# A delta rule's decay matrices as fp32r products of a fixed mask and split decays, four tiles in one matmul

## The chip, the cores and the metric

The kernel runs on one core of a Trainium2 chip. The metric is the device time of one execution in microseconds (us), here the median of 3 runs. The core has TensorE (PE: matmuls; PEld: its weight loads), VectorE (DVE), ScalarE (ACT), GpSimd (POOL) and SyncE (SP, which only issues DMAs). Each engine works through its own list of instructions in order; engines wait for one another by semaphores.

## The reference

A two-layer encoder over two sequences of 256 tokens each. Each layer has three branches side by side: latent attention, a gated linear recurrence (RG-LRU) and a gated delta rule with 4 heads, forward and backward; then a feed-forward part. The change lies in the delta rule alone. For each head and direction the log decays `g` of a chunk of 64 tokens are summed, and the exponentials of their differences scale the products of keys and queries:

```python
g = jnp.cumsum(chunks(g), axis=-1)
decay = jnp.exp(jnp.where(tril, g[..., :, None] - g[..., None, :], -jnp.inf))
A = jnp.where(strict, jnp.einsum('nbhid,nbhjd->nbhij', kb, k) * decay, 0.0)
T = lax.linalg.triangular_solve(eye + A, jnp.broadcast_to(eye, A.shape), left_side=True,
                                lower=True, unit_diagonal=True)
attn = jnp.einsum('nbhid,nbhjd->nbhij', q, k) * decay
q_dec = q * jnp.exp(g)[..., None]
```

The kernel works on tiles of 128 tokens (four tiles for both sequences) instead of chunks of 64.

## The kernel before

**Work and order.** Activations lie transposed, 128 channels on the partitions and 512 tokens (both sequences) in the columns. Nearly all of the time goes to products with weights, each done as three fp32r matmuls of 128x512 (`wh`,`wl` and `hh`,`hl` are the high and low parts of weight and activation). The weights come by DMA in pieces of 128x1024 (`raw`); ACT makes `wh` and DVE makes `wl`. Beside this stream the delta rule, the recurrence and the attention run as generators. PE's order is fixed when the program is built: a `Driver` keeps a virtual clock that each emitted matmul moves on, and a generator that has yielded a time (table `SLACK`) is taken up again when the clock has passed it. The orders of DVE, ACT, POOL and SP are made by the framework's scheduler from the whole program, so that they move when the program does.

**The part that changes** is the first half of `solve(h)`, run for 4 heads in each of 2 layers. For each direction DVE scales a strict triangular mask by the decays of the four tiles (`gw`, 128x512, L1317), and PE multiplies each tile of it with the inclusive mask, in fp32, four 128x128 products into `gdn_z` (L1326). ACT takes the exponential (`E`). For the decay of the queries DVE fills a third `gw` with the decays (two operations of 128x256, L1335) and PE does four more fp32 products into `gdn_eg` (L1340). The tile `gw` has two buffers.

**What follows in a head.** The products of keys and queries (`gdn_gram`, L1352) are scaled on DVE into `B`. The 16x16 diagonal blocks of `B` go to POOL by way of DRAM (`cb`, `dl`, `Lb`), where 30 operations (`xt`, `X`, L1381 and L1382) invert them; the result goes back by way of DRAM (`dx`) into `W`, which DVE transposes (L1392, L1393). Products on PE then join the blocks to 32 (`gdn_l16`: two stages, `W` added to at L1421 and transposed at L1422), to 64 (`gdn_l32`, two stages) and to 128 columns (`gdn_l64`, two stages); a trace names all of these `gdn_l`. POOL copies the parts of `W` into `XF` and `Y` (L1439, L1438), DVE copies the last part of `Y` (L1475), and the recurrence over tiles (`gdn_rec`) uses `Y`. The next head's diagonal blocks are inverted on POOL while this head is joined.

**What shares the engines with it.** In the stretch of head 1, the RG-LRU puts long scans and products on DVE (`rs`, `ru`, `xc`, `gsq`), and splits `xc` into `xch` (POOL, recorded at L308) and `xcl` (DVE, L298). Two helpers record most of the operations: L220 all matmuls, L292, L295, L298 and L301 those of DVE and POOL.

Of the kernel before, what the change touches and what calls it, by code (L numbers as in the profile page):

```python
# [8 lines left out]
F32 = mybir.dt.float32  # L9
F32R = mybir.dt.float32r  # L10
# [3 lines left out]
ALU = mybir.AluOpType  # L14
# [4 lines left out]
P = 128  # L19
# [60 lines left out]

CC = {}
_n = 0
for _name, _w in [("ident", 128), ("ones", 128), ("incf", 128), ("incb", 128), ("strf", 128),
                  ("strb", 128), ("sel1", 2), ("sel2", 4), ("sel4", 8), ("off16", 64)]:
    CC[_name] = (_n, _w)
    _n += _w
NCC = _n


def constants():  # L90
# [144 lines left out]
def _body(es, tc, nc, xT, cT, wall, wmod, pvec, fng, cst, rope, xinit, yT, dbg):  # L235
    V, A, G = nc.vector, nc.scalar, nc.gpsimd
    drv = Driver()
    PE = Tensor(nc.tensor, drv)
    depth = pvec.shape[1]

    cp = es.enter_context(tc.tile_pool(name="const", bufs=1))
    sp = es.enter_context(tc.tile_pool(name="small", bufs=1))
# [8 lines left out]

    def fill(pool, size):
        return pool.tile([P, size // 4], F32, name="fill", tag="fill", bufs=1)
    fill(sp, 160)


    cs = cp.tile([P, NCC], F32, name="cs")
    nc.scalar.dma_start(cs, cst)

    def C(name):  # L260
        o, w = CC[name]
        return cs[:, o:o + w]
# [5 lines left out]
    ident, ones = C("ident"), C("ones")  # L268
# [351 lines left out]
    xs, h = [], {}  # L620
    start = ExitStack()
    stp = start.enter_context(tc.tile_pool(name="start", bufs=1))
    c_raw = stp.tile([P, 8, 32], F32, name="c_raw")
    nc.sync.dma_start(c_raw, cT)
    t1 = stp.tile([P, 8, 32], F32, name="c_t")
# [8 lines left out]
    for k in range(8):  # L634
        t = xp.tile([P, T], F32, name="x", tag="x")
# [8 lines left out]
    for k in range(8):  # L644
        t = stp.tile([P, T], F32, name="sq", tag="t", bufs=4)
# [31 lines left out]
    for l in range(depth):  # L677
# [342 lines left out]
        for job in JOBS:  # L1020
# [91 lines left out]
            elif k == "out":  # L1112
                d, g = ix
# [25 lines left out]
            elif k == "down":  # L1139
                d, g = ix  # L1140
# [16 lines left out]
                t = x1[d]  # L1157
# [29 lines left out]
class GDN:  # L1187
# [16 lines left out]
    def gates(self, ab):  # L1204
# [14 lines left out]
        fl = "p a b -> p (a b)"  # L1219
        self.softplus(self.g.rearrange(fl), al.rearrange(fl), 32)  # L1220
        V.tensor_tensor(self.g, self.g, nea, ALU.mult)
        yield SLACK["softplus"]

        pc = self.aux_tile((P, 4, 16), "gates")
# [76 lines left out]
    def solve(self, h):  # L1301
# [10 lines left out]
        gt = self.g.rearrange("p t e -> p e t")  # L1312


        def scaled(mask, cols):
            w = g2.tile([P, 4, P], F32, name="gw", tag="gw", bufs=2)
            V.tensor_tensor(w, mask.unsqueeze(1).to_broadcast([P, 4, P]), self.bc(cols, P), ALU.mult)  # L1317
            return w

        ws = [scaled(C(strict[d]), gt[:, 4 * d + h, :]) for d in range(2)]  # L1320
        yield SLACK["ws"]
        E = []
        for d in range(2):
            pz = self.aux_tile((P, 4, P), "gdn_z")
            for t in range(4):
                PE.matmul(pz[:, t, :], ws[d][:, t, :], C(inc[d]), start=True, stop=True)  # L1326
            e = g2.tile([P, 4, P], F32, name="E", tag="E", bufs=4)
            A.activation(e, pz, AF.Exp)
            E.append(e)
            if d == 0:  # L1330
                yield SLACK["z"]

        w = g2.tile([P, 4, P], F32, name="gw", tag="gw", bufs=2)
# [347 lines left out]
```

## Time and profile before

| what | value |
|---|---|
| median of 3 runs | 2039.64 us (2038.04 to 2040.38) |
| the profiled execution | 2038.05 us |
| its span in the trace | 2036.3 us |
| PE busy | 1980.2 us, 97% |
| DVE, ACT, POOL busy | 1249.8, 808.7, 254.7 us |
| mean granted TensorE clock | 0.983 |

The span runs from the first to the last instruction; the execution's own time is 1.75 us longer. Busy time counts instructions that do work; an engine can also stand between them, waiting for another one. The granted clock is the share of the full TensorE clock (2.4 GHz) that PE had.

### The profile page before, as it was taken

How to read it: one execution, taken by the hardware profiler on the slowest of the kernel's cores; microseconds unless marked ns; L12 is line 12 of the kernel's file. 1: busy time of each engine (PE TensorE's matmuls, PEld its weight loads, DVE VectorE, ACT ScalarE, POOL GpSimd, SP SyncE). 2: the span in 40 equal slices, each digit the busy share in tenths (PEclk: the TensorE clock that was granted, in tenths of full speed). 3: DMA queues.
4: the chain of work that ended last, by engine and by line, in shares of the span. 5: the costliest groups of instructions: out<-in, count | busy, mean ns of one | idle time of the engine just before them, and what ended most of it. 6: DMA issues, size and time to landing. Idle time of an engine off the chain costs nothing.

```text
span 2036.3 us, 28679 instructions
## 1 busy us (share of the span) xinstructions
PE 1980.2 (97%) x11179; PEld 1561.3 (77%) x11179; DVE 1249.8 (61%) x2354; ACT 808.7 (40%) x1259; POOL 254.7 (13%) x519
## 2 busy tenths in 40 slices
PE   9999989999999999999999999799999999999998
PEld 4777756767887778888878777577778878888887
DVE  5675767744466766662367757785544667666434
ACT  3454355422333434442234534553323344444322
POOL 1100252222100100000011003523130010000000
PEclk9999989999999999999999999899999999999999
DMA  7232433334335343344334224333442533333333
GB/s 300 83 94 63 118 86 100 108 112 117 88 117 194 114 135 102 94 142 153 114 109 108 59 77 114 92 114 85 127 111 82 207 104 102 95 94 104 94 95 112
DMA packets 114135, 229.94 MB, mean 113 GB/s; under 512 B 52304, under 2 KB 57552, under 8 KB 114000
## 3 DMA queue, kind: packets, MB, share of 16 engines
q1 hardware_dynamic: 107376, 219.98, 36.2%
q10 hardware_dynamic: 6624, 8.14, 1.2%
q8 instruction: 88, 1.44, 0.3%
q14 instruction: 47, 0.39, 0.1%
HBM read 221.00 MB, written 7.08 MB: 112 GB/s over the span
## 4 chain that ended last, share of the span: by engine, by line
PE 83%; DVE 5%; POOL 5%; DMA 3%; issue 2%; ACT 2%; SPq 1%; POOLq 0%; DVEq 0%; ACTq 0%
PE mm_up L220 24%; PE mm_down L220 12%; PE mm_gate L220 11%; PE mm_br L220 6%; PE mm_out L220 4%; PE mm_in L220 3%; PE mod L220 3%; PE mm_z L220 2%; PE mm_gk L220 2%; PE mm_gv L220 2%; POOL xt L292 2%; POOL X L298 2%; PE mm_gq L220 2%; PE att_s L220 1%; PE gdn_rec L220 1%
## 5 line engine op out<-in xcount | busy, mean ns | idle before, releaser
L298 DVE TENSOR_TENSOR wl<-raw,wh 128x1024 fp32r<-128x1024 f32 x304 | 374.6, 1232 | 307.5 <-ACT wh L387 301.8
L387 ACT CAST wh<-raw 128x1024 fp32r<-128x1024 f32 x304 | 319.0, 1050 | 533.2 <-PE mm_down L220 126.9
L220 PE MATMUL mm_up<-hh,wh 128*128 128x512 f32 x704 | 276.4, 393 | 3.5 <-POOL hh L308 3.5
L220 PE MATMUL mm_up<-hl,wh 128*128 128x512 f32 x704 | 275.4, 391 | 0.0
L220 PE MATMUL mm_up<-hh,wl 128*128 128x512 f32 x704 | 275.0, 391 | 0.0
L301 DVE SCALAR_TENSOR_TENSOR cv<-mm_up,pv,cv 128x510 f32<-128x510 f32 x176 | 131.2, 748 | 68.5 <-ACT cv L550 65.4
L220 PEld LDWEIGHTS mm_up<-hh,wh 128*128 128x128 f32 x704 | 132.9, 189 | 38.0 <-issue 5.9
L220 PE MATMUL mm_gate<-hh,wh 128*128 128x512 f32 x384 | 160.6, 418 | 0.0
L220 PEld LDWEIGHTS mm_up<-hl,wh 128*128 128x128 f32 x704 | 132.9, 189 | 27.8 <-DVE hl L298 0.4
L220 PEld LDWEIGHTS mm_up<-hh,wl 128*128 128x128 f32 x704 | 132.9, 189 | 27.8
L220 PE MATMUL mm_gate<-hh,wl 128*128 128x512 f32 x384 | 150.2, 391 | 0.0
L220 PE MATMUL mm_gate<-hl,wh 128*128 128x512 f32 x384 | 149.9, 390 | 0.0
L220 PE MATMUL mm_down<-ah,wl 128*128 128x512 f32 (+1 forms) x396 | 144.8, 366 | 0.5 <-DVE wl L298 0.5
L220 PE MATMUL mm_down<-ah,wh 128*128 128x512 f32 (+1 forms) x396 | 144.9, 366 | 0.0
L220 PE MATMUL mm_down<-al,wh 128*128 128x512 f32 (+1 forms) x396 | 144.7, 365 | 0.0
L308 POOL TENSOR_SCALAR hh<-hn 128x256 fp32r<-128x256 f32 x64 | 34.0, 544 | 689.2 <-ACT hn L567 686.8
L550 ACT ACTIVATE cv<-mm_up,pv 128x512 f32<-128x512 f32 x88 | 68.5, 780 | 93.4 <-PE mm_up L220 93.4
L220 PEld LDWEIGHTS mm_gate<-hh,wh 128*128 128x128 f32 x384 | 72.2, 188 | 25.5 <-issue 12.5
L220 PEld LDWEIGHTS mm_gate<-hh,wl 128*128 128x128 f32 x384 | 72.1, 188 | 16.2
L220 PEld LDWEIGHTS mm_down<-ah,wl 128*128 128x128 f32 x396 | 74.7, 189 | 12.7 <-DVE wl L298 0.7
L220 PEld LDWEIGHTS mm_down<-ah,wh 128*128 128x128 f32 x396 | 74.7, 189 | 12.1
L220 PEld LDWEIGHTS mm_down<-al,wh 128*128 128x128 f32 x396 | 74.7, 189 | 12.0
(389 smaller groups left out, 3869.4 us busy)
## 6 DMA issues: line engine op xcount, KB each, us to landing
raw<-in_wall_dram SPq DMA_DIRECT2D x304, 512.0 KB, 3.6
raw<-in_wmod_dram SPq DMA_DIRECT2D x56, 512.0 KB, 3.6
mraw<-in_wmod_dram SPq DMA_DIRECT2D x16, 512.0 KB, 10.0
oraw<-in_wmod_dram SPq DMA_DIRECT2D x16, 512.0 KB, 7.3
hraw<-in_wmod_dram SPq DMA_DIRECT2D x16, 256.0 KB, 5.3
x<-in_xT_dram SPq DMA_DIRECT2D x8, 256.0 KB, 5.6
xr<-in_xT_dram ACTq DMA_DIRECT2D x8, 256.0 KB, 3.5
xdram<-x ACTq DMA_DIRECT2D x16, 128.0 KB, 2.5
```

What stands on the lines that cost most here:

```text
L220: return self.pe.matmul(out, lhsT, rhs, **kw)
L292: (eng or V).tensor_tensor(out, a, b, ALU.mult)
L298: (eng or V).tensor_tensor(out, a, b, ALU.subtract)
L301: V.scalar_tensor_tensor(out, a, s, b, op0, op1)
L308: G.tensor_scalar(hi, x, 1.0, 0.0, ALU.mult, ALU.add)
L387: A.copy(wh, raw)
L550: A.activation(dst, ps, AF.Identity, bias=bias, scale=w[lo])
```

## The change

The log decays `g` (128x32 for all heads) are split once in a layer into two fp32r parts, by two small operations on DVE; the high part takes the place of a tile that is free by then (`al_`). In `solve` the mask that is scaled is now the inclusive one, by each part (four DVE operations of 128x512 for a head). The other factor is the fixed strict mask, so one matmul of 512 columns does four tiles: two fp32r matmuls (high and low part) for `gdn_z` of a direction, and two of 256 columns with a matrix of ones for half of `gdn_eg`, from the same `gw`. Ones and strict masks are therefore needed in fp32r: they move to the end of the table of constants, come by a DMA of their own and are rounded into `mk` by one operation on POOL. The yields `z`, `gw` and `eg` are gone; `ws` is passed once in each direction.

```diff
@@ constants, _body
+    cs = cp.tile([P, NCC - NMASK], F32, name="cs")
+    nc.scalar.dma_start(cs, cst[:, 0:NCC - NMASK])
+    mk = cp.tile([P, NMASK], F32R, name="mk")
...
+    m_raw = stp.tile([P, NMASK], F32, name="m_raw")
+    nc.scalar.dma_start(m_raw, cst[:, NCC - NMASK:])
+    G.tensor_scalar(mk, m_raw, 1.0, 0.0, ALU.mult, ALU.add)
@@ gates
         V.tensor_tensor(self.g, self.g, nea, ALU.mult)
+        self.gs = [al.bitcast(F32R), sp.tile([P, 4, 8], F32R, name="g_l", tag="g_l")]
+        V.tensor_copy(self.gs[0], self.g)
+        self.sub(self.gs[1], self.g, self.f32(self.gs[0]))
         yield SLACK["softplus"]
@@ solve
-        ws = [scaled(C(strict[d]), gt[:, 4 * d + h, :]) for d in range(2)]
-        yield SLACK["ws"]
         E = []
+        pe = self.aux_tile((P, 4, P), "gdn_eg")
         for d in range(2):
+            ws = []
+            for x in self.gs:
+                w = g2.tile([P, 4, P], F32R, name="gw", tag="gw", bufs=2)
+                V.tensor_tensor(w, C(inc[d]).unsqueeze(1).to_broadcast([P, 4, P]),
+                                self.bc(self.f32(x).rearrange("p t e -> p e t")[:, 4 * d + h, :], P), ALU.mult)
+                ws.append(w)
+            yield SLACK["ws"]
             pz = self.aux_tile((P, 4, P), "gdn_z")
-            for t in range(4):
-                PE.matmul(pz[:, t, :], ws[d][:, t, :], C(inc[d]), start=True, stop=True)
+            for i, w in enumerate(ws):
+                PE.matmul(pz, C(strict[d], F32R), w, start=(i == 0), stop=(i == 1))
+            for i, w in enumerate(ws):
+                PE.matmul(pe[:, 1 - d::2, :], C("ones", F32R), w[:, 1 - d::2, :], start=(i == 0), stop=(i == 1))
             e = g2.tile([P, 4, P], F32, name="E", tag="E", bufs=4)
             A.activation(e, pz, AF.Exp)
             E.append(e)
-            if d == 0:
-                yield SLACK["z"]
-
-        w = g2.tile([P, 4, P], F32, name="gw", tag="gw", bufs=2)
-        for d in range(2):
-            V.tensor_tensor(w[:, 1 - d::2, :], self.ones.unsqueeze(1).to_broadcast([P, 2, P]),
-                            self.bc(gt[:, 4 * d + h, 1 - d::2], P), ALU.mult)
-        yield SLACK["gw"]
-        pe = self.aux_tile((P, 4, P), "gdn_eg")
-        for t in range(4):
-            PE.matmul(pe[:, t, :], w[:, t, :], C(inc[1 - t % 2]), start=True, stop=True)
```

The change also moves work on the engines whose order the scheduler makes. Line numbers after the change are 1 to 6 higher at most places.

The first place is on DVE, in the stretch of head 1 of layer 0, where `W` (head 0's inverse blocks) is transposed. Before:

```order
L298 TENSOR_TENSOR wl<-raw,wh 128x1024
L298 TENSOR_TENSOR xcl<-xc,xch 128x512
L301 SCALAR_TENSOR_TENSOR rs<-rm,rs 128x512
L911 MEMSET ra 128x2
L1335 TENSOR_TENSOR gw<-cs,g__763 128x2x128
L910 MEMSET rs 128x2
L1335 TENSOR_TENSOR gw<-cs,g__763 128x2x128
L1317 TENSOR_TENSOR gw<-cs,g__763 128x512
L1392 STREAM_TRANSPOSE W<-W 128x128
L1393 STREAM_TRANSPOSE W<-W 128x128
L1317 TENSOR_TENSOR gw<-cs,g__763 128x512
```

and now:

```order
L301 TENSOR_TENSOR wl<-raw,wh 128x1024
L1393 STREAM_TRANSPOSE W<-W 128x128
L301 TENSOR_TENSOR xcl<-xc,xch 128x512
L1394 STREAM_TRANSPOSE W<-W 128x128
L304 SCALAR_TENSOR_TENSOR rs<-rm,rs 128x512
L917 MEMSET ra 128x2
L1330 TENSOR_TENSOR gw<-cs,al__766 128x512
L916 MEMSET rs 128x2
L1330 TENSOR_TENSOR gw<-cs,g_l 128x512
L1330 TENSOR_TENSOR gw<-cs,al__766 128x512
L1330 TENSOR_TENSOR gw<-cs,g_l 128x512
```

The `gw` that finish head 1 stood ahead of the two transposes; now the first two of the four, which are head 1's second direction, stand behind both (the last two are head 2's first).

The second place is PE's order for head 1, which uses those `gw`. Before, from the second `gdn_z`:

```order
L220 MATMUL gdn_z<-cs,gw 128x128 x4
L220 MATMUL mod<-raw,csil 32x512 x2
L220 MATMUL mm_g<-hh_460,wh 128x512
...
L220 MATMUL mm_g<-hh_550,wl 128x512
L220 MATMUL gdn_eg<-cs,gw 128x128 x4
L220 MATMUL mm_b<-xch,wh 128x512
```

and now, from the first:

```order
L221 MATMUL gdn_z<-gw,mk 128x512 x2
L221 MATMUL gdn_eg<-gw,mk 128x2x128 x2
L221 MATMUL mm_g<-hh_452,wh 128x512
...
L221 MATMUL mm_g<-hh_554,wl 128x512
L221 MATMUL gdn_z<-gw,mk 128x512 x2
L221 MATMUL gdn_eg<-gw,mk 128x2x128 x2
L221 MATMUL mm_b<-xch,wh 128x512
```

Both products of the second direction now stand where `gdn_eg` alone stood, behind the last `mm_g` of that piece.

The third place is POOL, at head 1's inversion (`xt` and `X`), where `xch` is a part of the RG-LRU that DVE's `xcl` waits for. Before, `xch` stood behind the whole inversion:

```order
L298 TENSOR_TENSOR X<-X,xt 128x8x2
L292 TENSOR_TENSOR xt<-Lb,X 128x8
L298 TENSOR_TENSOR X<-X,xt 128x8
L308 TENSOR_SCALAR xch<-xc 128x512
L882 TENSOR_SCALAR gsq<-gsq 128x512
```

and now it stands in it, 13 operations from its end:

```order
L295 TENSOR_TENSOR xt<-Lb,X 128x8x8
L301 TENSOR_TENSOR X<-X,xt 128x8x8
L295 TENSOR_TENSOR xt<-Lb,X 128x8x7
L311 TENSOR_SCALAR xch<-xc 128x512
L301 TENSOR_TENSOR X<-X,xt 128x8x7
```

## Rows read from the trace of the kernel before

**Rows 1.** The page: busy time of the engines; the chain that ended last, by engine.

```profile
PE 1980.2 (97%) x11179; PEld 1561.3 (77%) x11179; DVE 1249.8 (61%) x2354; ACT 808.7 (40%) x1259; POOL 254.7 (13%) x519
...
PE 83%; DVE 5%; POOL 5%; DMA 3%; issue 2%; ACT 2%; SPq 1%; POOLq 0%; DVEq 0%; ACTq 0%
```

**Rows 2.** PE's waits: engine and line, releaser: us in total, times, longest.

```profile
PE gdn_l L220 <- DVE W L295: 12.3, 2, 6.3
PE gdn_rec L220 <- DVE Y L1475: 10.7, 2, 5.6
...
PE gdn_l L220 <- DVE W L1392: 3.4, 2, 1.7
```

**Rows 3.** PE's timeline, head 0, layer 0: start us, us of the row, instruction.

```profile
218.60 0.39 PE L220 MATMUL mm_gq<-hh,wl 128*128 128x512 f32 x1
218.83 1.05 PE L220 MATMUL gdn_z<-cs,gw 128*128 128x128 f32 x8
...
220.19 0.39 PE L220 MATMUL mm_gq<-hh,wl 128*128 128x512 f32 x1
```

**Rows 4.** PE's timeline in the last matmuls, of 256 columns.

```profile
2009.75 0.28 PE L220 MATMUL mm_down<-ah,wl 128*128 128x256 f32 x1
...
2011.91 0.28 PE L220 MATMUL mm_down<-ah,wl 128*128 128x256 f32 x1
```

**Rows 5.** Groups of the tile gw with shapes apart: ns min/median/max; here layer 0.

```profile
L1317 DVE TENSOR_TENSOR gw<-cs,g__763 x8: 650/686/693, 216.2 to 382.7; 128x512 f32<-128x512 f32 x8
L1335 DVE TENSOR_TENSOR gw<-cs,g__763 x8: 398/418/424, 220.4 to 474.3; 128x256 f32<-128x256 f32 x8
```

**Rows 6.** PE's timeline at the start of the program.

```profile
13.26 1.05 PE L220 MATMUL ssq<-cs,acc 128*128 128x1 f32 x8 [0.65 <-DVE acc L295]
```

**Rows 7.** PE's timeline, head 1; idle before in brackets.

```profile
262.96 1.16 PE L220 MATMUL gdn_eg<-cs,gw 128*128 128x128 f32 x8 [0.72 <-DVE gw L1335]
...
283.36 0.65 PE L220 MATMUL gdn_l<-W,B 32*32 32x32 f32 x32 [6.26 <-DVE W L295]
...
286.80 0.26 PE L220 MATMUL gdn_l<-vs,W 32*32 32x32 f32 x1
...
308.23 1.62 PE L220 MATMUL gdn_rec<-vt,Y 128*128 128x128 f32 x6 [5.11 <-DVE Y L1475]
```

**Rows 8.** DVE's timeline, head 1's stretch.

```profile
266.47 0.31 DVE L1393 STREAM_TRANSPOSE W<-W 128x128 f32<-128x128 f32 x1 [0.39 <-DMA W<-dx]
...
267.27 0.68 DVE L292 TENSOR_TENSOR qd<-qd,kq 128x512 f32<-128x512 f32 x1
...
283.82 0.44 DVE L1422 STREAM_TRANSPOSE W<-W 128x256 f32<-128x256 f32 x1
...
306.88 0.69 DVE L298 TENSOR_TENSOR xcl<-xc,xch 128x512 fp32r<-128x512 f32 x1 [6.91 <-POOL xch L308]
...
307.65 0.43 DVE L1475 COPY Y<-gdn_l 64x256 f32<-64x256 f32 x1
```

**Rows 9.** Windows: busy us (x instructions) of each engine, granted clock, DMA share, GB/s.

```profile
283.40:289.40 6.00, 6.00 (x91) 4.45 (x92) 4.25 (x7) 3.52 (x8) 5.47 (x9) 0.50 0.36 42
...
308.20:311.00 2.80, 2.77 (x10) 1.54 (x10) 2.25 (x3) 1.06 (x2) 0.00 (x0) 0.50 0.27 50
311.00:314.00 3.00, 3.00 (x9) 1.92 (x8) 3.00 (x4) 0.63 (x1) 0.28 (x1) 0.59 0.92 251
```

**Rows 10.** POOL's timeline in the same stretch.

```profile
287.20 5.20 POOL L1438 TENSOR_SCALAR Y<-W 32x128 f32<-32x128 f32 x8
292.48 0.46 POOL L292 TENSOR_TENSOR xt<-Lb,X 128x120 f32<-128x120 f32 x1
...
301.48 0.32 POOL L292 TENSOR_TENSOR xt<-Lb,X 128x56 f32<-128x56 f32 x1
...
306.23 0.62 POOL L308 TENSOR_SCALAR xch<-xc 128x512 fp32r<-128x512 f32 x1
```

More of the change, by code (lines that the diff above doesn't have):

```diff
@@ L82 @@
 _n = 0
-for _name, _w in [("ident", 128), ("ones", 128), ("incf", 128), ("incb", 128), ("strf", 128),
-                  ("strb", 128), ("sel1", 2), ("sel2", 4), ("sel4", 8), ("off16", 64)]:
+for _name, _w in [("ident", 128), ("incf", 128), ("incb", 128), ("sel1", 2), ("sel2", 4), ("sel4", 8),
+                  ("off16", 64), ("ones", 128), ("strf", 128), ("strb", 128)]:
     CC[_name] = (_n, _w)
@@ L87 @@
 NCC = _n
+NMASK = 3 * P
 def constants():
@@ L253, in fill, with C @@
         return pool.tile([P, size // 4], F32, name="fill", tag="fill", bufs=1)
[L254 to L260, printed above, removed]
+    fill(sp, 32)
+    cs = cp.tile([P, NCC - NMASK], F32, name="cs")
+    nc.scalar.dma_start(cs, cst[:, 0:NCC - NMASK])
+    mk = cp.tile([P, NMASK], F32R, name="mk")
+    def C(name, dtype=F32):
         o, w = CC[name]
-        return cs[:, o:o + w]
+        o -= NCC - NMASK
+        return mk[:, o:o + w].bitcast(dtype) if o >= 0 else cs[:, CC[name][0]:CC[name][0] + w]
     pv = cp.tile([P, depth, NPV], F32, name="pv")
@@ L1311, in solve @@
         inc, strict = ("incf", "incb"), ("strf", "strb")
-        gt = self.g.rearrange("p t e -> p e t")
-        def scaled(mask, cols):
-            w = g2.tile([P, 4, P], F32, name="gw", tag="gw", bufs=2)
-            V.tensor_tensor(w, mask.unsqueeze(1).to_broadcast([P, 4, P]), self.bc(cols, P), ALU.mult)
-            return w
-        ws = [scaled(C(strict[d]), gt[:, 4 * d + h, :]) for d in range(2)]
-        yield SLACK["ws"]
         E = []
+        pe = self.aux_tile((P, 4, P), "gdn_eg")
         for d in range(2):
+            ws = []
[5 more added lines that the diff above has]
+            yield SLACK["ws"]
             pz = self.aux_tile((P, 4, P), "gdn_z")
-            for t in range(4):
-                PE.matmul(pz[:, t, :], ws[d][:, t, :], C(inc[d]), start=True, stop=True)
+            for i, w in enumerate(ws):
+                PE.matmul(pz, C(strict[d], F32R), w, start=(i == 0), stop=(i == 1))
+            for i, w in enumerate(ws):
+                PE.matmul(pe[:, 1 - d::2, :], C("ones", F32R), w[:, 1 - d::2, :], start=(i == 0), stop=(i == 1))
             e = g2.tile([P, 4, P], F32, name="E", tag="E", bufs=4)
@@ L1329, in solve @@
             E.append(e)
-            if d == 0:
-                yield SLACK["z"]
-        w = g2.tile([P, 4, P], F32, name="gw", tag="gw", bufs=2)
-        for d in range(2):
-            V.tensor_tensor(w[:, 1 - d::2, :], self.ones.unsqueeze(1).to_broadcast([P, 2, P]),
-                            self.bc(gt[:, 4 * d + h, 1 - d::2], P), ALU.mult)
-        yield SLACK["gw"]
-        pe = self.aux_tile((P, 4, P), "gdn_eg")
-        for t in range(4):
-            PE.matmul(pe[:, t, :], w[:, t, :], C(inc[1 - t % 2]), start=True, stop=True)
         qd = g2.tile([P, 4, P], F32, name="qd", tag="qd", bufs=2)
```

## The prediction

> **What bounds the kernel now.** The page comes first: PE is busy for 97% of the span, and 83% of the chain that ended last is PE's [rows 1]. So a matmul taken out shortens the run as long as PE does not wait instead. The list of PE's waits comes next, because a faster stretch can only be worth what the wait behind it lets through. Two of its longest lie in the delta rule: the joining of blocks to 32 waits 12.3 us for DVE's sum `W`, once in each layer, and the recurrence waits 10.7 us for DVE's copy of `Y`, again once in each layer [rows 2]. In layer 0 they stand at 283.36 (6.26 us) and 308.23 (5.11 us) [rows 7]; both belong to heads 0 and 1, and layer 1 repeats layer 0 some 1004 us later. Last I read windows behind the two waits, for the granted clock: 0.50 from 283.4 to 289.4, 0.50 from 308.2 to 311.0 and 0.59 from there to 314.0, with PE busy throughout [rows 9]. A wait of five to six microseconds thus costs about three more at the lower of the two levels, 1.2 GHz. These four waits and their tails are where the change's effect is decided, since it moves what stands in front of them on DVE and POOL.
>
> **Matmuls removed and added.** A `gdn_z` of four fp32 products: from the `mm_gq` at 218.60 to the one at 220.19 are 1.59 us, in which three matmuls of 512 columns start too. One of those takes 0.23 us (218.60 to 218.83) [rows 3], so the products add 1.59 - 3 x 0.23 = 0.90 us. A head has three such groups (two `gdn_z` and `gdn_eg`, which has the same shapes): 2.7 us. In their place come four matmuls of 512 columns at 0.23 us, and four of 256. For these the row is the last `mm_down`: 18 steps in 2.16 us, 0.12 us each [rows 4]. That is 0.92 + 0.48 = 1.40 us. A head saves 1.3 us of PE, eight heads 10.4 us.
>
> **DVE.** Before, a head scales two masks of 128x512 and two of 128x256: 2 x 0.69 + 2 x 0.42 = 2.2 us. Now four of 128x512: 2.75 us [rows 5], 0.55 us more. I take the fp32r output at the price of the fp32 one; lower bound 0, as DVE is idle in much of the program, upper bound 0.55 x 8 = 4.4 us where every one lay on the path. Heads 0 and 1 are walked through below, with their DVE work counted; for heads 2 and 3 I charge 0.5 us a layer. The split of `g` is two operations of 128x32 in a layer, each below the 0.42 us of 128x256, beside a weight stream on PE: nothing (at most 1.7 us in all).
>
> **The start.** Ones in fp32r are wanted first by `ssq` at 13.26 us, where PE waits for DVE's sum anyway [rows 6]. The bytes loaded are the same, in two pieces, and POOL's rounding of 128x384 is shorter than its 0.62 us for 128x512 [rows 10]. I take nothing; if it were late, by its own length, 0.6 us.
>
> **Head 1, where the order moves.** Before, `gdn_eg` waited 0.72 us and began at 262.96, so PE was there at 262.24 [rows 7]. Now it comes there earlier by head 0's 1.3 us, and by 1.1 us of head 1 itself (two `gdn_z`, 1.8 us, are replaced by one half of the new work, 0.7 us): at 259.8. What it needs are the `gw` of the second direction, and these now stand on DVE behind both transposes of head 0's `W`. The second of them ended at 266.78 (266.47 + 0.31) [rows 8], after the blocks had come back from POOL by way of DRAM. Everything upstream (PE's `gdn_gram`, POOL's inversion, the DMAs) can be earlier by head 0's 1.3 us, and somewhat more, as `Lb` moves ahead of a weight load in SP's queue. Bounds: 266.8 with no lead, 263.5 with all of it and 2 us from the queue; I take 265.0, nearer the lead. Then `rs` and two `gw`, 0.65 us each, make 267.0. So a **new wait of 7.2 us** (5.7 to 9.0) in place of 0.7. Queued behind it on PE are `mm_b`, the `gdn_gram` of head 1 and `gdn_l`; queued behind the next `gw` pair on DVE, which needs the buffers that these matmuls free, is all that leads to the old wait.
>
> **From there to the joining to 32.** The first buffer comes free after three of PE's four matmuls, at half clock about 2 x 0.46 + 0.24 = 1.1 us; two more `gw` end at 267.0 + 1.1 + 1.3 = 269.4. Before, DVE began the work that follows at 267.27, and the transpose of the summed `W` (L1422) at 283.82, 16.55 us later [rows 8]. The list in between is the same but for one `xcl` more, 0.69 us, which waits for POOL; I take 1.5 us for that wait (0 to 2.5, the order of POOL's pieces). L1422 then ends near 269.4 + 16.55 + 0.7 + 1.5 + 0.44 = 288.6. The sum `W` itself now stands ahead of the scans, so the wait for it goes, but the second stage, at 286.80 before [rows 7], needs the transpose and becomes the place of the wait: about 288.7, 1.9 us late. Before, 2.6 us of half clock were left there (286.8 to 289.4); now a stretch of 6.0 us follows the wait in full: (6.0 - 2.6) x 0.5 = 1.7 us more. PE is **3.6 us late** (0 to 6.4).
>
> **The recurrence.** Before, PE reached it at 308.23 - 5.11 = 303.12 and waited for the copy of `Y` [rows 7], which on DVE stood behind `xcl`, idle 6.91 us for POOL's `xch` [rows 8]; and `xch` stood behind the whole inversion, which ended at 306.23 [rows 10]. Now `xch` is met within it, behind the `xt` of 128x56: (301.48 - 292.48) + 0.32 = 9.3 us from the inversion's first operation. POOL's eight pieces of `Y` take 287.20 to 292.48, 5.3 us [rows 10], and can begin at 288.6. So `xch` ends at 288.6 + 5.3 + 9.3 + 0.6 = 303.8, and `xcl`, two memsets and the copy (306.88 to 308.08, 1.2 us [rows 8]) end at 305.0. PE arrives at 303.1 + 3.6 = 306.7: **no wait**, 1.5 us ahead of before. And the half clock behind it isn't paid: 2.8 x 0.50 + 3.0 x 0.41 = 2.6 us [rows 9]. Together 4.1 us ahead. Bounds, from those above: 7.1 ahead, or 1.3 late where all of them are late and the wait stays.
>
> A rule of the Trainium skill speaks against taking the first new wait so lightly: the page "TensorE: Matmul & The Clock Gate", section "HAM oscillation — how this bites in real kernels", says that a matmul stream with gaps drops to the lower clock after each of them and pays the way back each time. The trace agrees, with 0.50 behind the 6.26 us wait. In my sum the half clock behind the new wait costs nothing, since PE waits again for DVE at the end of that stretch; by the rule alone it would be 3.0 us a layer, and the forecast 2033.
>
> **Heads 2 and 3.** Their order moves little. Head 3 gains its 1.3 us. In head 2 PE waits 1.7 us in a layer for `W`'s transposes [rows 2], and this joining now stands two triples of `mm_z` later; I take 1.3 us (0 to 1.7).
>
> **Sum.** A layer: -4.1 - 1.3 - 1.3 + 0.5 = -6.2 us; two layers -12.4. The profiled execution took 2038.05 us, so 2025.7; the median lies 1.6 us above that execution, so **2027**.
>
> **Rivals.** *Only the arithmetic counts*: the waits change places and keep their length in sum. Then -10.4 us, 2029. For it: new and old waits are of like length (7.2 against 6.3). Against: the half clock is then as long as before only by chance. *Swallowed*: `Y`'s copy ends between 308 and 310, so the second wait stays with its half clock, and heads 0 and 1 give nothing (0 to 2.1 us lost in a layer), against 2.1 us gained in heads 2 and 3: 2035 to 2040, say 2038. For it: DVE and POOL make the times there, not PE, and they have more to do. Against: `xch` moves by some four microseconds, and the copy with it. *Slower*: the new wait is given back nowhere. A layer then pays 7.2 - 0.7 = 6.5 us and 3.0 us of half clock, less 4 x 1.3: +4.3 us, in two layers +8.6, 2048. It decides from the point at which `Y`'s copy ends after 310.3, 5.3 us later than I work out: the layer's loss there is then more than the 2.1 us of heads 2 and 3. A DVE that stands for PE's buffers in more places than I count would do it.
>
> **How the numbers follow.** Chances: the forecast 0.48 (its own range 2020 to 2034), arithmetic alone 0.20, swallowed 0.17, slower 0.15. About 0.2%, 4 us, is what a measurement of this kernel can tell from no change. The first two are faster: 0.68; swallowed is mostly the same, 0.16, and slower holds the rest, 0.16. The best bounds in heads 0 and 1 are 6 us below the forecast, 2021, and heads 2 and 3 can add little more: low 2018. Upward the range takes in swallowed and most of slower: 2046.
>
> **What would show it.** Right: the `gdn_z` groups as two records of 128x512 at a step of 0.23 us; a wait of 6 to 9 us of `gdn_z` for `gw` in head 1; no wait for `W` at L295 but one of about 5 us in the second stage; the wait of `gdn_rec` for `Y` gone, and the clock near 1.00 behind it. Wrong: a wait for `Y` that stays or grows, a clock of 0.50 behind two waits in a layer that PE does not win back, or new waits for `gw` in heads 0, 2 and 3.

## The result, and the profile after

| | before | after |
|---|---|---|
| median, 4 runs each on one chip | 2038.84 us (2037.85 to 2040.38) | 2076.12 us (2072.15 to 2079.24) |
| the profiled execution | 2038.05 us | 2072.15 us |
| its span | 2036.3 us | 2070.0 us |
| mean granted TensorE clock | 0.983 | 0.975 |

The ratio is 1.0185 [1.0173, 1.0197]: the change makes the kernel 37 us slower. The forecast was 2027 with a range up to 2046, so both its direction and its range are wrong.

The page after, in the two lines that answer to [rows 1]: busy time, and the chain that ended last, by engine.

```profile
PE 1982.3 (96%) x11051; PEld 1556.4 (75%) x11051; DVE 1249.0 (60%) x2358; ACT 807.3 (39%) x1259; POOL 260.5 (13%) x520
...
PE 78%; POOL 7%; DVE 5%; issue 4%; DMA 3%; ACT 2%; SPq 1%; POOLq 0%; DVEq 0%; ACTq 0%
```

PE has 128 instructions fewer and is busy no less, at a lower mean granted clock (0.975 for 0.983). POOL's share of the chain rises from 5% to 7%. The list of PE's waits, which answers to [rows 2]:

```profile
PE gdn_rec L221 <- ACT Ss L1491: 15.5, 2, 7.8
PE gdn_z L221 <- DVE rs L916: 13.0, 2, 6.7
PE gdn_l L221 <- DVE W L1423: 12.1, 2, 6.0
PE mm_z L221 <- ACT wh L390: 8.2, 4, 3.0
...
PE mm_z L221 <- DVE wl L301: 3.7, 4, 1.5
```

Each stands once or twice in a layer. PE's own timeline in layer 0 (start, us of the row, instruction, idle before in brackets), to be held against [rows 7]:

```profile
268.16 1.41 PE L221 MATMUL gdn_z<-gw,mk 128*128 128x512 f32 x2 [6.72 <-DVE rs L916]
...
291.29 0.23 PE L221 MATMUL gdn_l<-vs,W 32*32 32x32 f32 x1 [6.04 <-DVE W L1423]
...
308.99 0.91 PE L221 MATMUL gdn_rec<-vt,Y 128*128 128x128 f32 x6 [1.11 <-POOL X L301]
...
325.16 2.07 PE L221 MATMUL gdn_rec<-Ss,kq 128*128 128x128 f32 x8 [7.68 <-ACT Ss L1491]
...
527.24 0.50 PE L221 MATMUL mm_z<-hh,wh 128*128 128x512 f32 x1 [3.04 <-ACT wh L390]
...
528.50 0.79 PE L221 MATMUL mm_z<-hh,wl 128*128 128x512 f32 x1 [0.52 <-DVE wl L301]
```

The first three were forecast: the new wait for `gw`, the joining's wait moved to its second stage, and next to nothing left of the wait for `Y`. (In two of them the profile names a neighbour: the first `gw` ended at 268.11, beside a memset of `rs`, and the copy of `Y` ended 0.03 us ahead of POOL's `X`.) The last three were not. How far PE is behind the kernel before, taken from the start of the same matmul in both traces (counted by name; us, minus is ahead), follows. Each column is counted from its own first `mm_in`, at 23.1 us, long before the delta rule: the traces of the three experiments are 1.7, 2.0 and 0.7 us late there already, that of the change 0.0.

| matmul (start before) | after | one_part_old_order | same_work_old_order | loads_first_h1_h3 |
|---|---|---|---|---|
| 22nd mm_g (261.4) | -0.9 | -2.7 | +3.5 | -0.5 |
| 7th mm_b (263.9) | +5.9 | -2.0 | +2.2 | +7.0 |
| 70th mm_x (293.1) | +4.9 | -2.1 | +1.6 | +5.5 |
| 76th mm_x (313.1) | -2.0 | -1.9 | +1.0 | -1.3 |
| 34th mm_b (323.4) | +8.0 | -2.1 | +0.7 | +0.3 |
| 1st mm_z (426.3) | +9.3 | -3.9 | -0.8 | -0.1 |
| 400th mm_gate (503.9) | +8.7 | -5.9 | -3.6 | -1.6 |
| 61st mm_z (519.8) | +16.6 | -5.8 | -3.6 | -1.4 |

(The three experiments are told below.) Until 313 us the change stood as forecast, 2.0 us ahead. It then lost 10.0 us at one place, where the recurrence waits for `Ss`, and 7.9 us at another, in head 3's stretch, where PE waits for weights. Layer 1 repeats both.

**The first loss** is followed back from `Ss`, which ACT copies. ACT's timeline:

```profile
319.46 0.63 ACT L887 ACTIVATE gsq<-gt 128x512 f32<-128x512 f32 x1 [8.19 <-DMA dx<-X]
321.65 1.04 ACT L390 CAST wh<-raw 128x1024 fp32r<-128x1024 f32 x1 [1.55 <-DMA raw<-in_wall_dram]
322.71 1.28 ACT L890 ACT_TABLE_LOAD   x1
324.00 0.63 ACT L890 ACTIVATE gsq<-gsq 128x512 f32<-128x512 f32 x1
324.54 0.57 ACT L1491 COPY Ss<-gdn_rec 128x512 f32<-128x512 f32 x1
```

The copy stands behind the cast of a weight, and the cast waits for its load. Before, the same cast (the 38th of `in_wall`) waited for PE and not for its load, and the copy came straight behind it:

```profile
315.32 1.05 ACT L387 CAST wh<-raw 128x1024 fp32r<-128x1024 f32 x1 [1.69 <-PE mm_x L220]
317.13 0.59 ACT L1490 COPY Ss<-gdn_rec 128x512 f32<-128x512 f32 x1 [0.76 <-PE gdn_rec L220]
```

ACT's order has moved too: a table load and `gsq`, 1.9 us, now stand between cast and copy, where they stood behind the copy. SP's queue, which issues the loads (start, us to issue):

```profile
315.87 1.81 SPq L1387 DMA_DIRECT2D dx<-X  x4
317.79 0.38 SPq L381 DMA_DIRECT2D raw<-in_wall_dram  x1
```

and the same queue before:

```profile
306.30 1.81 SPq L1386 DMA_DIRECT2D dx<-X  x4
309.40 0.35 SPq L378 DMA_DIRECT2D raw<-in_wall_dram  x1
```

Before as after, the load stands behind the four `dx` of head 1's inversion, and SP issues nothing in the last 8 us of that inversion (before) or the last 14 (after). With 37 loads of `in_wall` ahead of `dx` in both, it is the end of the inversion that moved, by 9.6 us. POOL's timeline, against [rows 10]:

```profile
296.43 0.47 POOL L295 TENSOR_TENSOR xt<-Lb,X 128x120 f32<-128x120 f32 x1
...
300.85 0.31 POOL L1399 MEMSET XF<- 128x256 f32 x1 [1.00 <-PE gdn_l L221]
...
306.64 0.32 POOL L295 TENSOR_TENSOR xt<-Lb,X 128x56 f32<-128x56 f32 x1
306.92 0.62 POOL L311 TENSOR_SCALAR xch<-xc 128x512 fp32r<-128x512 f32 x1
...
308.94 1.30 POOL L295 TENSOR_TENSOR xt<-Lb,X 128x40 f32<-128x40 f32 x1
310.32 0.27 POOL L301 TENSOR_TENSOR X<-X,xt 128x40 f32<-128x40 f32 x1
...
312.33 1.04 POOL L301 TENSOR_TENSOR X<-X,xt 128x24 f32<-128x24 f32 x1
...
315.63 0.22 POOL L301 TENSOR_TENSOR X<-X,xt 128x8 f32<-128x8 f32 x1
```

It starts 3.9 us later than the 292.48 of before, behind the late second stage, and takes 19.4 us (296.43 to 315.85) for 13.8. Up to the `xt` of 128x56 the difference is 1.2 us (10.2 for 9.0), with a wait of 1.00 for PE in it (the memset of `XF`). From there to the end it is 4.5 us (9.2 for 4.75): `xch` itself, 0.6, and operations that are several times as long as their neighbours, 1.30 us for the `xt` of 128x40 against 0.27 for the `X` of that size. DVE's timeline shows what ran beside them:

```profile
307.57 0.78 DVE L301 TENSOR_TENSOR xcl<-xc,xch 128x512 fp32r<-128x512 f32 x1 [3.75 <-POOL xch L311]
...
308.41 0.43 DVE L1476 COPY Y<-gdn_l 64x256 f32<-64x256 f32 x1
308.87 1.23 DVE L301 TENSOR_TENSOR wl<-raw,wh 128x1024 fp32r<-128x1024 f32 x1
...
312.07 2.38 DVE L926 TENSOR_TENSOR_SCAN rs<-ra,ru 128x512 f32<-128x512 f32 x2
```

Before, DVE stood still for 6.91 us there, waiting for `xch` behind the inversion [rows 8]. With `xch` inside, DVE goes on, and its `wl` (308.87 to 310.10) runs beside nearly all of the long `xt` (308.94 to 310.24). The Trainium skill's page "SBUF — State Buffer", section "SBUF: two separate sides", states that a GpSimd operation that reads SBUF and a VectorE operation with two SBUF inputs lock one another out for a whole instruction; the two rows agree with that.

**The second loss** is a cast again, and SP's list shows it (head 3, layer 0), before:

```profile
498.83 7.21 SPq L378 DMA_DIRECT2D raw<-in_wall_dram  x3
515.36 1.81 SPq L1386 DMA_DIRECT2D dx<-X  x4
```

and after, with the cast on ACT that waits for the load behind `dx`:

```profile
511.05 0.33 SPq L381 DMA_DIRECT2D raw<-in_wall_dram  x1
520.36 1.81 SPq L1387 DMA_DIRECT2D dx<-X  x4
522.27 0.39 SPq L381 DMA_DIRECT2D raw<-in_wall_dram  x1
...
526.14 1.04 ACT L390 CAST wh<-raw 128x1024 fp32r<-128x1024 f32 x1 [9.81 <-DMA raw<-in_wall_dram]
```

Counted over SP's list, 61 loads of `in_wall` stood ahead of head 3's `dx` and now 59 do; for heads 0, 1 and 2 the counts are 33, 37 and 48 in both. Two loads that had been issued by 506 us now wait for an inversion that ends at 520. The windows behind the two losses (us, busy time and instructions of PE, PEld, DVE, ACT, POOL, granted clock, DMA share, GB/s):

```profile
325.10:328.20 3.10, 3.04 (x11) 2.85 (x12) 2.55 (x5) 0.01 (x1) 0.96 (x1) 0.50 0.46 148
328.20:331.00 2.80, 2.80 (x9) 1.92 (x9) 1.78 (x5) 1.80 (x3) 0.00 (x0) 0.69 0.06 23
...
527.20:530.20 3.00, 2.44 (x6) 1.71 (x7) 1.45 (x2) 1.22 (x2) 0.00 (x0) 0.62 0.56 160
530.20:533.20 3.00, 3.00 (x12) 2.71 (x12) 1.67 (x5) 0.80 (x2) 0.00 (x0) 0.50 0.97 333
533.20:536.20 3.00, 3.00 (x68) 2.49 (x69) 0.75 (x1) 0.00 (x0) 0.00 (x0) 0.74 0.39 154
```

Behind `Ss` PE loses 3.04 x 0.50 + 2.80 x 0.31 = 2.4 us to the lower clock, so 7.7 + 2.4 = 10.1 us against the 10.0 of the table. In head 3 it is 3.6 us of waits and 2.44 x 0.38 + 3.00 x 0.50 + 3.00 x 0.26 = 3.2 us, 6.8 of the 7.9.

### The profile page after: what moved, and what is told of

It reads as the page before. It is cut to its first block, busy times and chain, and to the rows that moved or that the text cites. A ratio compares the mean times of both kernels' runs of the same rounds, so it can differ in the third digit from the quotient of the medians.

```text
span 2070.0 us, 28424 instructions
## 1 busy us (share of the span) xinstructions
PE 1982.3 (96%) x11051; PEld 1556.4 (75%) x11051; DVE 1249.0 (60%) x2358; ACT 807.3 (39%) x1259; POOL 260.5 (13%) x520
## 4 chain that ended last, share of the span: by engine, by line
PE 78%; POOL 7%; DVE 5%; issue 4%; DMA 3%; ACT 2%; SPq 1%; POOLq 0%; DVEq 0%; ACTq 0%
PE mm_up L221 23%; PE mm_down L221 12%; PE mm_gate L221 9%; PE mm_br L221 6%; PE mm_out L221 4%; PE mm_in L221 3%; PE mod L221 3%; POOL xt L295 3%; POOL X L301 2%; PE mm_z L221 2%; PE mm_gk L221 2%; PE att_s L221 1%; PE gdn_rec L221 1%; PE mm_gv L221 1%; PE mm_gq L221 1%
## 5 line engine op out<-in xcount | busy, mean ns | idle before, releaser
L221 PE MATMUL mm_up<-hh,wl 128*128 128x512 f32 x704 | 274.9, 390 | 0.0
L221 PEld LDWEIGHTS mm_gate<-hh,wl 128*128 128x128 f32 x384 | 72.1, 188 | 16.6 <-DVE wl L301 0.3
## 6 DMA issues: line engine op xcount, KB each, us to landing
mraw<-in_wmod_dram SPq DMA_DIRECT2D x16, 512.0 KB, 10.1
```

The lines of the kernel that those rows point to most:

```text
L221: return self.pe.matmul(out, lhsT, rhs, **kw)
```

## The experiments

The theory: the loss comes from the order, from what stands on other queues behind a late inversion. The rival: it comes from the added work itself, on DVE and PE. Where an expectation speaks of A and B, these are the theories of that run. The edits are to the changed kernel, and ratios are to the kernel before on the same chip.

### x_by_pool

The trace names `dx` as what ACT waited for at 319.46: the DMA that refills `X` is issued by ACT and must wait until `dx` has read it. Here POOL issues it.

```diff
-        nc.scalar.dma_start(X, self.xinit)
+        nc.gpsimd.dma_start(X, self.xinit)
```

> The changed kernel, with X's initial values loaded by a DMA that POOL issues instead of ACT; the order of everything else stays. In the changed kernel ACT stood 8.2 us at this DMA (it waits until head 1's X has been read out) and the copy of the state Ss, which PE waited 7.7 us for, stood behind it. Theory A, ACT's list is the cause: the wait of gdn_rec for Ss goes, with the half clock behind it, about 9 us in each layer; 2076 becomes 2058. Theory B, the inversion on POOL is late (19.4 us long, where it was 13.8) and holds DVE's list as well, where the transposes of W stand ahead of xc, xcl and r: PE then waits for xcl or r instead, until about 326, and only 2 to 3 us in a layer are won: 2070 to 2074.

2078.17 us, 1.0193 [1.0177, 1.0209]. PE waits for `Ss` for 7.70 us, as without the edit, and ACT's own wait has moved to the cast (timelines of SP and ACT):

```profile
318.65 1.81 SPq L1387 DMA_DIRECT2D dx<-X  x4
320.57 0.38 SPq L381 DMA_DIRECT2D raw<-in_wall_dram  x1
...
324.46 1.04 ACT L390 CAST wh<-raw 128x1024 fp32r<-128x1024 f32 x1 [7.62 <-DMA raw<-in_wall_dram]
```

So ACT's DMA is not the cause; two things waited for one inversion, and the load behind `dx` on SP is the later. Neither theory held: A's gain is missing, and so are B's waits for `xcl` or `r`.

### dx_by_pool_h3

Head 3's `dx` and `W` go through POOL's queue, so that no load stands behind them.

```diff
+        q = nc.gpsimd if h == 3 else nc.sync
...
-            nc.sync.dma_start(dx.rearrange(...
+            q.dma_start(dx.rearrange(...
```

> The changed kernel, with head 3's six DMAs of dx and W issued by POOL instead of SP; no weight load stands behind them any more. In the changed kernel SP stood at dx until 520.4 and the weight loads behind it landed so late that PE waited 5 to 6 us for wh and wl of mm_z, part of it followed by half clock; the difference to the kernel before grew there from 7.7 to 16.6 us. Theory A, SP's order is the cause: these waits go and about 8 us in each layer with them: 2059 to 2062. Theory B, the weights are late for another reason (buffers that come free late, or casts): the waits stay and the time is within 4 us of 2076.

2088.64 us, 1.0243 [1.0226, 1.026]: worse. The load comes in time, but DVE's `wl` stands behind the transposes of `W`, which wait longer (timelines of POOL, DVE and PE):

```profile
526.27 2.53 POOL L1388 DMA_DIRECT2D dx<-X  x4 [0.31 <-POOL X L301]
...
533.10 0.31 DVE L1394 STREAM_TRANSPOSE W<-W 128x128 f32<-128x128 f32 x1 [9.38 <-DMA W<-dx]
...
535.37 0.80 PE L221 MATMUL mm_z<-hh,wl 128*128 128x512 f32 x1 [5.28 <-DVE wl L301]
```

The same late inversion blocks a second list, DVE's. Taking one queue out of its way is not enough, and the time is above what either theory had.

### gw_first and w_sum_first

The first puts the four `gw` ahead on DVE, which takes away the forecast's new wait; the second also puts the sum of `W` and its transposes ahead.

```diff
+                with self.tc.high_priority():
                     V.tensor_tensor(w, C(inc[d])...
...
+        with self.tc.high_priority():                    # w_sum_first alone
             self.add(W[:, 0], W[:, 0], pw)
             V.transpose(W[:, 1], W[:, 0])
```

> The changed kernel, with the scaled masks given priority on DVE: head 1's second pair stands ahead of the transposes of W again, as it did before the change. The new wait of gdn_z (6.7 us in a layer) goes to 1 us or less. Theory A, this wait is given back later, as the prediction had it (at 315 us the changed kernel was 1.2 us ahead in spite of it): the stretch to 315 us gains 2 to 4 us in a layer and the waits behind it stay: 2068 to 2076. Theory B, the wait and the half clock behind it are the root of the lateness of POOL's inversion, and so of the waits behind: 2045 to 2057.

> As gw_first (2072), with priority also for the sum W and its transpose (L1423) on DVE: two operations lie between them in head 1's stretch, where it were sixteen. Theory A, the late transpose is the root: the wait of 5.3 us in the second stage of the joining to 32 goes, with part of the half clock behind it; POOL's pieces of Y and head 1's inversion start earlier, and so do the weight loads that stand behind the inversion in SP's list, whose lateness is the 7.7 us wait at 325 us: 2045 to 2060. Theory B, the inversion is bound by its own input (B, cb, Lb, made late on DVE), and by DVE's work beside it: it still ends after 313, the wait at 325 stays, and the time is 2063 to 2072.

2072.19 us, 1.0169 [1.015, 1.0187], and 2075.10 us, 1.0185 [1.017, 1.0201]. With `gw_first`, counted as in the table above, the wait of `gdn_z` is gone (-1.4 us at the 7th mm_b in place of +5.9), but PE is at +6.3 by the 46th mm_g (274.9), where the change is at +6.7, and the second stage still waits 5.3 us and `Ss` 7.8. With `w_sum_first` the second stage no longer waits, but `wl` stands in its place (4.57 us), the inversion ends at 318.8, and `Ss` waits 6.9. The new waits in front are real and are not the loss: what takes them away pays at the next one. That is theory A of `gw_first`, in its range, and theory B of `w_sum_first`, 3 us above its range; neither time is clear of the change's by its interval.

### xch_behind

A one-column operation ties `xch` behind head 1's inversion again.

```diff
+            if i == 2:
+                G.tensor_scalar(xh[:, 0:1], gdn.X[:, 7, 15:16], 1.0, 0.0, ALU.mult, ALU.add)
             split(xc, xh, xl, pool=True)
```

> The changed kernel, with the xch that had moved into head 1's inversion on POOL tied behind it again, by one operation of one column that reads the end of the inversion. Theory A: xch in the middle released DVE's work (xcl, wl, v, ru, the scans) into the second half of the inversion, whose 13 last operations then took 8.4 us where they took 3.9; tied behind, the inversion ends near 311 instead of 315.9, DVE's copy of Y a little later, and the wait of gdn_rec for Ss falls from 7.7 to some 3 us: 2064 to 2070. Theory B, the inversion is slow for another reason (its late start, the memset of XF within it): it ends at 314 or later, the copy of Y is later on top, and the time is 2076 or more.

2073.40 us, 1.0169 [1.0154, 1.0184]. The inversion takes 14.9 us (298.91 to 313.84) in place of 19.4, and the wait for `Ss` is gone (its copy no longer stands behind a cast that waits for that load). So the lengthening comes from `xch` and the DVE work that it lets run. But DVE's list is now late, and PE waits for it:

```profile
320.54 0.79 PE L221 MATMUL mm_x<-hh,wl 128*128 128x512 f32 x1 [4.46 <-DVE wl L301]
```

At the 34th mm_b (323.4) PE is 4.7 us behind in place of 8.0, counted as in the table, and head 3 loses 7.5 us where the change loses 7.9. Theory A was right on the inversion; the time lies between the two theories, and it isn't clear of the change's.

### one_part_old_order and one_part_new_order

Both leave out the low part of the split decays, and so half of the new products. The first keeps the yields of the kernel before and moves the virtual clock as the old products did, so that PE's list stays as it was and the others nearly so; the second is the changed kernel without the low part.

```diff
+        ws = [scaled(C(inc[d]), gt[:, 4 * d + h, :]) for d in range(2)]    # one_part_old_order
+        yield SLACK["ws"]
...
+            old(4 * 4 * 0.42 * P * 1e-3)
...
-            for x in self.gs:                                               # one_part_new_order
+            for x in self.gs[:1]:
```

> The arithmetic of the change in one part alone (the low part of the decays is left out), with the yields and PE's virtual times of the kernel before, so that PE's order is that of before and the lists of the other engines differ in a few rows. A head's three fp32 groups (2.7 us of PE) become two matmuls of 512 columns and two of 256 (0.7 us); DVE's work is that of before. Theory A, the arithmetic is worth what was worked out and the changed order alone makes the changed kernel slow: 2.0 us a head and 16 us in all, less what the two old waits take back in heads 0 and 1 (up to 4 us a layer): 2023 to 2031. Theory B, the fp32r products themselves make something slow (their writes, their weight loads, the fp32r scaling on DVE): no faster than 2039.

> The changed kernel without the low part of the decays (one scaled mask, one matmul for z and one for half of eg in a direction; the low part is left out): the yields of the change stay, so that z and eg of a direction stand together on PE, but both directions' masks fit into the two buffers of gw and DVE makes 1.4 us a head instead of 2.75. 59 weight loads stand ahead of head 3's dx, as in the changed kernel (61 in the kernel before). Theory A, the place of the products and the loads' order are the cause: above 2055. Theory B, the second part is (its work on DVE and its wait for buffers): 2025 to 2040, except for the 6 to 9 us a layer at head 3, if the order of the loads makes these by itself: then 2037 to 2050.

2033.51 us (10 runs), 0.9983 [0.9972, 0.9994], and 2056.28 us, 1.0083 [1.0062, 1.0103]. The first lies between its two theories, and its gain is clear of no change; the second is in theory A, by 1 us. The two have the same products, the second has less work on DVE, and the order turns a gain of 4 us into a loss of 18. In the new order 59 loads stand ahead of head 3's `dx`, and it loses 7.3 us there. It isn't the change's order throughout: here `xch` stands behind head 1's inversion, which ends at 306.9, and PE doesn't wait for `Ss`. So the second loss comes without the low part; the first was seen only in kernels with both parts. In the old order the two waits of heads 0 and 1 are about as long as before (PE's waits):

```profile
PE gdn_rec L221 <- DVE Y L1490: 12.4, 2, 6.4
PE gdn_l L221 <- DVE W L298: 11.1, 2, 5.6
```

(10.7 and 12.3 us in [rows 2].) Two heads save 4.0 us of PE. By the table above PE is 2.1 us ahead behind heads 0 and 1, about half, and 5.9 by head 3: heads 2 and 3 pay out nearly in full.

### same_work_old_order

As many scalings and products as the change has, in the old order: each mask is scaled twice into the same tile, by the low part and then by the high, and each product is made twice. The low part is thus left out of the result.

```diff
+            for x in (self.gs[1], self.gs[0]):
+                V.tensor_tensor(w, mask.unsqueeze(1).to_broadcast([P, 4, P]), ...
...
+            for _ in range(2):
+                PE.matmul(pz, C(strict[d], F32R), ws[d], start=True, stop=True)
```

> All of the change's work in the order of one_part_old_order (2033.5): each mask is scaled twice, by the low and then by the high part, into the same tile, and each matmul runs twice, so that DVE has the same four operations of 128x512 and PE the same eight matmuls in a head as in the changed kernel; the low part's values are left out of the result. No operation waits for a buffer of the other direction. Theory A, the order alone made the loss: PE has 0.7 us a head more than in one_part_old_order and DVE 0.55 us: 2034 to 2041. Theory B, the additional work of DVE in heads 0 and 1 is the loss, as that stretch is bound by DVE: 2048 or more.

2036.55 us (10 runs), 0.9994 [0.9984, 1.0003]: no difference from before that can be measured, and about 40 us less than the change, as theory A had it. The added DVE work and products cost little in this order (0.9994 against 0.9983 with one part). What the change has beyond this kernel is its order and four scaled masks that share two buffers, and the loss goes with these two. PE waits 6.5 us for `W` and 4.5 for `Y` here; it is 0.7 us behind after heads 0 and 1, and 3.6 ahead by head 3.

### Four versions of the whole computation

Two keep the change's code and steer the order by yields and priorities: `old_order_two_parts` (with the tie of `xch_behind`) and `old_order_xch_inside` (without it). Two do all low-part products first and the high-part ones later, with other yields: `two_phases_a` and `two_phases_b`.

```diff
-            yield SLACK["ws"]
+            yield (3.0, 5.0)[d]                                   # the first two
...
+        ws = [scaled(d, self.gs[1]) for d in range(2)]            # the last two: low parts
...
+        ws = [scaled(d, self.gs[0]) for d in range(2)]            # and then the high ones
```

> The whole arithmetic of the change, with three changes to the order: priority for the scaled masks, xch tied behind head 1's inversion, and 5.0 in place of 3.0 us at the second direction's yield. As many weight loads now stand ahead of each dx in SP's list as in the kernel before (33, 37, 48, 61 in layer 0; 59 for head 3 in the changed kernel), the sum W and its transpose lie 2 operations apart (16), and the inversions are interrupted as before. Theory A, the order made the loss: a head saves 1.3 us of PE, less 0.55 us of DVE where DVE is late: 2026 to 2038. Theory B, the additional DVE work of the second part is the cause: it is all still there, and the time is above 2055.

> As old_order_two_parts (2047), without the tie: xch stands within head 1's inversion again. In old_order_two_parts the wait for Y's copy, behind xcl and xch, was 8.7 us in a layer. Theory A: xch within lets that copy go some 4 us earlier and the wait shrinks: 2039 to 2044. Theory B: DVE's work, let go earlier, slows the inversion's rest, and with it the weight loads behind dx: a wait for Ss or for weights comes back, 2047 to 2056.

> The whole computation of the change, high and low part, in nearly the order of the kernel before: the low parts of both directions go first (they fill the two buffers of gw and are multiplied into open accumulations), 2 us of PE's virtual time later the high parts follow at the places that z and eg had before; the yield kq is 2 us shorter, so that the high parts keep their time. The loads ahead of each dx are those of the kernel before. Theory A, the order decides: within 4 us of same_work_old_order, 2033 to 2041. Theory B, the second pass costs by itself (three accumulators stay open longer, and DVE's low masks stand in the dense stretch): 2044 or more.

> As two_phases_a, with 3 us between the passes and kq 3 us shorter; xch and XF stand within head 1's inversion here, and nothing of another part does in two_phases_a. Theory A, all that counts is the order at PE and SP, which is alike in the two: within 3 us of two_phases_a. Theory B, what lies within the inversion counts, as it lets DVE's work go early, which slows the rest of it: 5 us or more above two_phases_a.

| | time, us | ratio | behind at the 34th mm_b, from the first mm_in | lost from 400th mm_gate to 61st mm_z |
|---|---|---|---|---|
| old_order_two_parts | 2047.00 | 1.0046 [1.0031, 1.0061] | +4.5 | 0.0 |
| old_order_xch_inside | 2057.46 | 1.0090 [1.0074, 1.0105] | +2.6 | 0.0 |
| two_phases_a | 2050.69 | 1.0061 [1.0042, 1.0080] | +4.8 | 0.0 |
| two_phases_b | 2048.32 | 1.0049 [1.0034, 1.0064] | +3.9 | 0.0 |

All four have 61 loads ahead of head 3's `dx`, and none loses anything there. None beats the kernel before; they are 9 to 19 us slower than it, and each has waits of its own in the stretch of head 1. So the loads' order alone doesn't bring the time back, and the rival, that the second part costs by itself, isn't excluded: `two_phases_a` came out in its theory B, `old_order_two_parts` between its two, and `old_order_xch_inside` 1 us above its theory B. (`two_phases_b` is within 3 us of `two_phases_a`, its theory A.) The waits in `old_order_two_parts` are 7.3 us for `W`, 8.7 for `Y` and 3.5 for ACT's `gt`; in `old_order_xch_inside` the inversion is long again (17.2 us) and PE loses some 10 us more by 343 us, at `v`, `r` and `osq`; in `two_phases_a` they are 5.2 for `gt`, 5.0 for ACT's `rs` and 7.1 for `Y`. In `two_phases_b` the inversion ends at 315.5 and `Ss` waits 7.6 us, as in the change.

### loads_first_h3 and loads_first_h1_h3

Two one-column operations on POOL tie the end of head 3's inversion, or of head 1's and head 3's, behind a weight's load, so that SP issues that load ahead of `dx`; the yield `X` behind it is shorter by the time waited.

```diff
+        if h == 3:                          # the second: if h in (1, 3)
+            while len(self.gone) < {1: 38, 3: 61}[h] + 152 * self.l:
+                yield 0.5
...
+            self.sub(z, raw[:, 0:1], raw[:, 0:1], G)
+            self.add(X[:, 7, 15:16], X[:, 7, 15:16], z, G)
```

> The changed kernel; at head 3 two operations of one column on POOL tie the end of the inversion to the weight load of the next piece but one, so that 62 weight loads stand ahead of its dx in SP's list (59 in the changed kernel, 61 in the one before), and DVE's transposes of W stand behind the wl of those pieces. Theory A, the loads that stand behind head 3's dx make the loss at 527 us (the difference to the kernel before grows there from 10.3 to 16.6): it goes, 6 to 8 us in each layer, and 2076 becomes 2060 to 2064. Theory B, the loads are late there for another reason: 2070 or more.

> The same at head 1 too: 38 weight loads stand ahead of its dx (37 in the changed kernel and in the one before), at the same late end of the inversion. Theory A, the 7.7 us wait of gdn_rec at 325 us comes from the one weight load that stands behind dx, as ACT's cast of it stands ahead of the copy of Ss: the wait goes with its half clock, 8 to 9 us in a layer, beside those of head 3: 2043 to 2052. Theory B, the late inversion holds PE in more ways (DVE's transposes of W ahead of xc, xcl and r): another wait of like length comes in its place, and it is within 6 us of loads_first_h3.

2077.08 us, 1.0182 [1.0165, 1.0199], and 2053.58 us, 1.0069 [1.0051, 1.0087]. The first has 62 loads ahead of head 3's `dx`. From the 400th mm_gate to the 61st mm_z it loses 0.1 us in place of 7.9 (1.5 in place of 7.8 from the 48th mm_z on, as PE now waits 0.9 us for a weight ahead of that stretch): the wait is shown to come from the loads behind `dx`. Yet the time is that of the change, in theory B's range though the place bears out A. Head 3 is joined later, and PE waits for it where the branches meet, 2.3 us in each layer for `onx`, and again for `osq`. That gain was given back: counted from the first mm_in, PE is 12.3 us behind at the 61st mm_z and 17.9 when the feed-forward part begins (16.6 and 16.5 in the change).

With head 1's load ahead too (38 loads), SP and PE show the other loss gone. The inversion ends later than in the change, and PE hardly waits for `Ss` (timelines of SP and PE):

```profile
311.56 0.33 SPq L381 DMA_DIRECT2D raw<-in_wall_dram  x1
317.73 1.81 SPq L1397 DMA_DIRECT2D dx<-X  x4
...
320.33 1.16 PE L221 MATMUL gdn_rec<-Ss,kq 128*128 128x128 f32 x8 [1.42 <-ACT Ss L1502]
```

PE is 1.4 us ahead at the 61st mm_z, where the change is 16.6 behind, and the time falls by 22.5 us, 60% of the loss (theory A, 2 us above its range). Then PE waits at the joint again (2.05 for `osq` at 576.31, 2.32 for `onx` at 579.91) and is 5.3 us behind when the feed-forward part begins.

## Why the prediction was wrong, step by step

**The prices were right.** Head 0's `gdn_z` and half of `gdn_eg` take 0.69 us (218.85 to 219.54) for the 0.70 I had summed, and a `gw` takes 0.68 us in fp32r as in fp32.

**So was the walk to 313 us, in kind.** The new wait was forecast at 7.2 us and took 6.72, but its size is partly luck: PE came to it at 261.4 where I had 259.8, and the first `gw` was ready at 268.1 where I had 267.0. The sum `W` no longer holds PE up and the second stage does, from 291.29 where I had 288.7: the list behind the buffers took 2.6 us more. The wait for `Y`, 5.11 us, shrank to 1.11. PE was 2.0 us ahead at 313.1, forecast 4.1, with bounds from 7.1 ahead to 1.3 late. The clock rule that I set against this step didn't decide it: the granted clock was 0.50 behind the first wait (268.2 to 271.0), but PE waited again at 291.29, as I had argued.

**What failed is the end of "The recurrence" and the sentence "Heads 2 and 3. Their order moves little".** I followed `xch` into the inversion for what it gives to `Y`, and took the inversion's length over from before; "together 4.1 us ahead" was 8.0 us behind at 323.4. The inversion became 5.7 us longer, by `xch` and by the DVE work that `xch` releases, and it started late with the second stage. What is late next when the inversion is late I did not ask: SP's list has a weight load behind `dx`, ACT's list has the cast behind that load, and `Ss` behind the cast. In the trace of before there was slack: the load went out at 309.40, 5.9 us ahead of its cast, which waited for PE; after the change the cast came 3.9 us behind its load and waited for it. The inversion's 9.6 us used that slack up, ACT's new order added 1.9 us behind the cast, and 7.7 us of wait and 2.4 of half clock were left. `loads_first_h1_h3` shows this by putting that load ahead.

**For head 3 I read PE's and DVE's order and not SP's.** In place of its gain of 1.3 us the head lost 7.9. Two loads fewer stand ahead of its `dx`. Each kernel run here that has 59 loses 7.3 to 8.1 us at that place (`dx_by_pool_h3`, which took `dx` off SP, 10.3), and each that has 61 or 62 loses 0.1 or less.

**The rival "slower"** had a wrong mechanism: its first wait was given back, and `Y`'s copy ended at 308.84 (308.41 + 0.43), ahead of the 310.3 from which it was to decide. "Swallowed" is close to what `same_work_old_order` shows in the order of before: heads 0 and 1 give nothing (0.7 us lost), heads 2 and 3 do, and the time is that of before. No rival had a price for what the change lost.

**What stays open.** Of the 33.7 us between the two spans, the two places take 17.9 in a layer, less 2.0 that PE was ahead: 15.9, or 32 in both. That accounts for nearly all of the span; but an edit that undoes a loss does not give back its full size, because head 3's joining then ends the layer. What order would let the whole computation gain wasn't found. Whether the loss of 2.6 to 4.8 us at head 1 in the four versions is due to the two buffers of `gw` or to DVE's list wasn't separated, nor how much of the change's 37 us its order and how much the second part in two buffers costs: the order without the low part lost 18.

## What to carry to other kernels

When a change shifts the end of a long chain, list for every engine and queue what stands behind the first instruction that waits for it, DMA issues too: the price was a weight load on a third engine's queue and a copy on a fourth's. Compare SP's order as carefully as PE's; two loads on the other side of a blocked DMA cost more than all the products saved. And test a saving in the old order first: there half of the new products gained 4 us and as much work as the change has gained nothing that can be measured, so a new order had little to win and 37 us to lose.

## What the runs showed of the hardware

POOL's operations of 128x16 to 128x48 elements in an inversion took 0.2 to 0.3 us alone (the trace before, 302.4 to 305.7). In the changed kernel they took 0.6 to 0.7 us beside a DVE product or sum of 128x512 (0.7 to 0.8 us), and 1.0 to 1.3 beside `wl` of 128x1024 (1.23) or a scan (two in 2.38). So the length of a chain on POOL depends on what DVE is released to do beside it. Four small DMAs took 2.53 us to issue on POOL (`dx_by_pool_h3`) against 1.81 on SP.
